# One value projection and stick-breaking rounds in a written order, in the odd layer of a two-layer hybrid trunk

## The chip, the cores and the metric

The kernel runs on one core of one Trainium2 chip. The metric is the device time of one execution in microseconds (us), the median of several runs. The engines have short names here, as in the profile: PE (TensorE, the matmuls), DVE (VectorE), ACT (ScalarE), POOL (GpSimd) and SP (SyncE, which in this kernel issues DMAs only). ACT and POOL issue DMAs as well, each from its own queue.

## The reference

The trunk has two layers on 512 tokens of width 1024. Each is a mixer and a gated ConvFFN, both with a norm before and after and a residual. The change is in the mixer of the second ("odd") layer alone, which runs two kinds of attention side by side, with heads of 64 columns:

```python
def odd_mixer(h, w_in, w_out):
    cq, ck, cv, sq, sk, sv = split_cols(h @ w_in, ODD_SPLITS)   # 768, 768, 768, 256, 256, 256
    ...
    o_dil = dilated_attention(groups(cq), groups(ck), groups(cv), slopes)
    o_sb = stick_breaking_attention(heads_first(sq, SB_HEADS), heads_first(sk, SB_HEADS),
                                    heads_first(sv, SB_HEADS))
    return jnp.concatenate([heads_last(o_dil), heads_last(o_sb)], axis=-1) @ w_out
```

Dilated attention has three groups of four heads. Group 0 looks at a window of 128 tokens with step 1, group 1 at 512 with step 4, group 2 at 2048 with step 16; the three results of a head are merged by their softmax denominators. On 512 tokens, groups 1 and 2 connect tokens of the same residue modulo 4, so the kernel computes them on tokens reordered by residue r.

Stick-breaking attention has four heads. With strict causality it weighs a key by its own probability and by what all the keys between it and the query have left over, a reversed running sum:

```python
        z = jnp.einsum('bhqd,bhkd->bhqk', qblk, k).astype(jnp.float32) * scale
        log_beta = jax.nn.log_sigmoid(z)
        log_keep = jnp.where(strict, jax.nn.log_sigmoid(-z), 0.0)
        after = lax.cumsum(log_keep, axis=3, reverse=True) - log_keep
        a = jnp.where(strict, jnp.exp(log_beta + after), 0.0)
        return jnp.einsum('bhqk,bhkd->bhqd', a.astype(v.dtype), v)
```

## The kernel before

**Products in three parts.** All large products are made of float32 operands split in two: a high part (a cast to the fp32r type) and a low part (the difference). `mm3` (L316 to L320) makes three matmuls of them: high by high, high by low, low by high. A projection over the width of 1024 thus takes 8 k-steps (`KD`) of three matmuls.

**Weights.** The class `Weights` (L42 on) carries the list of all weight units in the order of their use (L207 to L216 for this layer), each 128 x 1024 float32. `load` (L54) issues the DMA of the next unit on SP's queue into one of three raw buffers (`wraw`). `split` (L82) casts it to `wh` on ACT (L83) and subtracts it into `wl` on DVE (L84); there are five buffers of each. `next` hands out the next pair and first sees to it that `depth` units from the present one are made; `ahead` makes units up to a given one. When a raw buffer is used again, its DMA waits in SP's queue until both readers of the earlier tile are done. A second instance `W2` handles the first two units of the output projection, with buffers of its own and the same raw buffers.

**Banks.** PSUM has eight banks, in tags: "a" three, "s" two, "t", "o" and "n" one each. `bank(tag, name)` takes the next of a tag and waits for the readers of its earlier use.

**Order.** Inside a `tc.manual_schedule` block the named engines run their instructions in the order in which the code writes them. Outside, a list scheduler places each instruction by its own estimate of when it becomes ready. SP is in none of the blocks of this function.

**The stages of `odd` (L1424 on), in order of time:**

1. The v12 projection (L1485 to L1504): values of groups 1 and 2, four row tiles of 128 tokens (order 3, 2, 1, 0), each 8 k-steps with 512 columns. ACT copies a finished tile to `vst`, and four DMAs on ACT's own queue scatter its rows by residue into `cv12`. Pieces of the layer before (`pending`) stand between its k-steps.
2. The projections of `sq` and `sk`, stick-breaking's queries and keys, transposed: `proj_T` (L1457), four units of 8 k-steps with 512 columns.
3. `proj_V(sv)` (L1467): stick-breaking's values, four row tiles with 256 columns, two units.
4. Two stick-breaking passes, each for a pair of heads (L1522 to L1600), with the eight projections `T12` of the dilated queries and keys of groups 1 and 2 among them, four in each pass. A pass has scores (PE, L1532), the mask's addition (DVE, L1536), min, Exp, Ln and max (L1542 to L1549), the split of the result in `sh` and `sl` (L226 and L227), and three rounds per head, j = 2, 1, 0. In a round PE adds the block sums into `run` (L1561) and the triangular sums into another bank `cp`, and DVE adds both to z (L1569, L1571); Exp follows for the finished columns on ACT (L1574). Last come the values (`osb`, L1580) and their split. There is one `sh` and one `sl`, so the two heads of a pass use them in turn. This stage stands outside any manual block.
5. In a manual block: the last four T-projections, with the scores of groups 1 and 2 (`score12`) between them; the exchange of softmax tops and sums through DRAM, on SP's queue (`exchange`).
6. `proj_V(cv)`: values of group 0, four row tiles with 256 columns, two units, with group 0's scores (`score0`) between.
7. The values stage: eight items, four of group 0 (`turn0`, `value0`) and four of groups 1 and 2 (`turn12`, `value12`). A turn transposes the softmax weights on PE (L1728) and ACT copies them to a buffer `pt` (L1729); the values add them up in the `oT` banks (L1677). `turned_to` picks the buffer for `pt` from three by the item's own number, so that both `turn0(0)` and `turn12(0, 0)` take the first. From the fifth turn of the loop on, `W.ahead` makes units ahead here: the last two of the output projection and three of the FFN's first.
8. The output projection (`ao`), a loop over four row tiles, with the norms and the FFN's transposes (`turned`) in it.

POOL meanwhile adds up the FFN's weights by accumulating DMAs (`make_sums`), from the end of stage 1 on.

Of the kernel before, what the change touches and what calls it, by code (L numbers as in the profile page):

```python
# [97 lines left out]
def trunk(tc, A, out):  # L98
# [3 lines left out]
    with ExitStack() as top:  # L102
# [1323 lines left out]
        def odd(xnT, pending, order):  # L1426
            xh, xl = xnT
            with ExitStack() as es:
# [4 lines left out]
                cv12 = ap.tile([P, 4, 512], F32, tag="cv12", name="cv12")  # L1433
# [8 lines left out]
                spare = [ap.tile([P, 4, 256], F32, tag=f"spare{n}", name="spare") for n in range(2)]  # L1442
# [4 lines left out]
                sv = sb.tile([P, NT, 256], F32, tag="sv", name="sv")  # L1447
# [4 lines left out]
                def proj_T(dst, scale, permuted, on_act):  # L1452
                    acc = bank("a", "apt")
                    wh, wl = W.next()
                    for k in range(KD):
                        mm3(acc[:], wh[:, k * P:(k + 1) * P], wl[:, k * P:(k + 1) * P],
                            xh[:, k], xl[:, k], k == 0, k == KD - 1)  # L1457
                    src, d = acc[:], dst[:]
# [3 lines left out]
                    if on_act:  # L1462
                        ACT.activation(d, src, AF.Copy, scale=scale)
                    else:
                        DVE.tensor_scalar(d, src, scale, None, ALU.mult)

                def proj_V(dst):  # L1467
                    ws = [W.next() for _ in range(2)]

                    def tile_V(i):  # L1470
                        t = slice(i * P, (i + 1) * P)
                        a = bank("a", "apv")
                        for k in range(KD):
                            wh, wl = ws[k // 4]
                            c = slice((k % 4) * 256, (k % 4 + 1) * 256)
                            mm3(a[:, :256], xh[:, k, t], xl[:, k, t], wh[:, c], wl[:, c], k == 0, k == KD - 1)
                        if i % 2:
                            DVE.tensor_copy(dst[:, i], a[:, :256])
                        else:
                            ACT.copy(dst[:, i], a[:, :256])  # L1480
# [5 lines left out]
                ws = [W.next() for _ in range(4)]  # L1486
                W.depth = 5
                for i in ORDER:
                    t = slice(i * P, (i + 1) * P)
                    a = bank("a", "av12")  # L1490
                    at, *parts = pending.pop(0) if pending else (KD, )
                    for k in range(KD):
                        if k == at:
                            for f in parts:
                                f()
                        wh, wl = ws[k // 2]
                        c = slice((k % 2) * 512, (k % 2 + 1) * 512)
                        mm3(a[:], xh[:, k, t], xl[:, k, t], wh[:, c], wl[:, c], k == 0, k == KD - 1)
                    if not pending:
                        W.ahead(W.pos + 1)  # L1500
                    st = chp.tile([P, 512], F32, tag="s", name="vst")
                    ACT.copy(st[:], a[:])
                    for r in range(4):
                        nc.scalar.dma_start(cv12[32 * i:32 * i + 32, r], st[r::4, :])  # L1504
# [6 lines left out]
                ACT.copy(lead[0:1, 1:2], st[0:1, 0:1])  # L1511
# [6 lines left out]
                tile_V = proj_V(sv)  # L1518
                for i in ORDER:
                    tile_V(i)  # L1520
# [3 lines left out]
                def sb_scores(u):  # L1524

                    zs = [sb.tile([P, 1280], F32, tag="z", name="z", bufs=2) for _ in range(2)]
                    for n, (j0, o0, o1) in enumerate(spans):
                        zp = [bank(t, "zp") for t in ("ss", "nt", "aa")[n]]
                        for j in (j0,) if j0 < 2 else (2, 3):
                            for y in range(2):  # L1530
                                r = slice(y * 64, y * 64 + 64)
                                PE.matmul(zp[y][:, off[j] - o0:off[j + 1] - o0], sk[u][r, j * P:(j + 1) * P],  # L1532
# [416 lines left out]
```

## Time and profile before

| What | us |
|---|---|
| Median of three runs | 1118.72 |
| The three runs | 1118.53, 1118.72, 1124.62 |
| The profiled execution | 1120.18 |
| Its span, first to last instruction | 1118.1 |
| Span of stages 1 to 8 (568.35 to 775.15) | 206.80 |
| Stage 1, v12 projection | 24.51 |
| Stage 5, last T-projections and scores | 27.07 |
| Stage 6, cv projection and scores of group 0 | 16.37 |
| Stage 8, output projection | 22.69 |

The profile is of one execution. The page gives busy time by engine first, then the span in 40 slices, the DMA queues, the chain of work that ended last, and the costliest groups of instructions; the trace answers finer questions, such as busy time by stretch, the waits of an engine, or its instructions in order of time. "L1561" is line 1561 of the kernel before. In a row of the timeline, what stands in square brackets is the idle time before it and what ended it. `out<-in` are the program's names. Matmuls are pipelined and their ends are modelled, so a busy PE may hold short waits.

### The profile page before, as it was taken

To read this page: it belongs to the slowest core of one execution; us is meant where nothing else is said; L and a number is where in the kernel's file an instruction comes from. 1 tells how busy PE (TensorE), PEld (TensorE's weight loads), DVE (VectorE), ACT (ScalarE), POOL (GpSimd) and SP (SyncE) were. 2 spreads that over 40 slices of the span, in tenths; PEclk is the share of its full clock that TensorE was granted. 3 is DMA by queue.
4 is the path that set the end of the run, shared out by engine and by line. 5 is a ranking of instruction groups with operands and counts; after the bars stand their busy time and mean duration, and the time that the engine had idled before them with its cause. 6 is when DMAs were issued, how large, how long until landed. Compare 5 with 4: busy or idle time off the path is not lost.

```text
span 1118.1 us, 18149 instructions
## 1 busy us (share of the span) xinstructions
PE 1105.9 (99%) x6792; PEld 961.6 (86%) x6792; DVE 898.6 (80%) x1509; ACT 641.9 (57%) x1091; POOL 126.2 (11%) x241
## 2 busy tenths in 40 slices
PE   9999999999999999999999999999999999999997
PEld 8876667898999999887888877888999999988876
DVE  6667676488899999999874566677899999999896
ACT  5555576346666665556543554565466666656562
POOL 2311143320000000000032111013200000000002
PEclk9999999999999999999999999999999999999999
DMA  8788898457556555354738999947656565535461
GB/s 289 239 227 228 224 283 219 126 181 199 170 180 196 173 187 180 123 179 150 245 95 280 289 293 289 238 115 201 201 155 199 173 187 191 173 126 164 151 207 75
DMA packets 72599, 218.02 MB, mean 195 GB/s; under 512 B 10048, under 2 KB 11200, under 8 KB 64320
## 3 DMA queue, kind: packets, MB, share of 16 engines
q1 hardware_dynamic: 61248, 147.53, 39.9%
q0 software_dynamic: 9920, 67.12, 24.0%
q10 hardware_dynamic: 1344, 2.23, 0.6%
q8 instruction: 53, 0.87, 0.3%
q14 instruction: 34, 0.28, 0.1%
HBM read 209.47 MB, written 73.43 MB: 253 GB/s over the span
## 4 chain that ended last, share of the span: by engine, by line
PE 76%; DMA 10%; DVE 8%; issue 4%; ACT 1%; POOL 1%; SPq 0%; POOLq 0%; DVEq 0%; ACTq 0%
PE u L320 12%; PE u L318 12%; PE u L319 12%; DMA ws<-in_ffn_up_q 5%; DVE wl L84 3%; DMA ws<-ws 3%; PE apt L318 3%; PE apt L319 3%; PE apt L320 3%; PE acc L318 3%; PE acc L320 2%; PE acc L319 2%; PE ao L318 2%; PE ao L320 2%; PE ao L319 2%
## 5 line engine op out<-in xcount | busy, mean ns | idle before, releaser
L84 DVE TENSOR_TENSOR wl<-wraw,wh 128x1024 fp32r<-128x1024 f32 x246 | 298.8, 1220 | 39.8 <-ACT wh L83 39.0
L83 ACT CAST wh<-wraw 128x1024 fp32r<-128x1024 f32 x246 | 254.8, 1047 | 111.8 <-PE u L319 24.4
L320 PE MATMUL u<-xh,wl 128*128 128x256 f32 (+1 forms) x640 | 195.0, 305 | 0.0
L318 PE MATMUL u<-xh,wh 128*128 128x256 f32 (+1 forms) x640 | 194.9, 305 | 0.0
L319 PE MATMUL u<-xl,wh 128*128 128x256 f32 (+1 forms) x640 | 194.8, 304 | 0.0
L320 PEld LDWEIGHTS u<-xh,wl 128*128 128x128 f32 x640 | 122.3, 191 | 5.5 <-DVE wl L84 0.7
L319 PEld LDWEIGHTS u<-xl,wh 128*128 128x128 f32 x640 | 122.3, 191 | 5.0
L318 PEld LDWEIGHTS u<-xh,wh 128*128 128x128 f32 x640 | 122.3, 191 | 4.9
L318 PE MATMUL u<-gh,wh 128*128 128x256 f32 x384 | 108.7, 283 | 0.0
L320 PE MATMUL u<-gh,wl 128*128 128x256 f32 x384 | 108.6, 283 | 0.0
L319 PE MATMUL u<-gl,wh 128*128 128x256 f32 x384 | 108.6, 283 | 0.0
L318 PE MATMUL acc<-wh,gh 128*128 128x512 f32 (+1 forms) x234 | 90.5, 389 | 0.6 <-DVE uu L689 0.6
L319 PE MATMUL acc<-wl,gh 128*128 128x512 f32 (+1 forms) x234 | 90.9, 388 | 0.0
L320 PE MATMUL acc<-wh,gl 128*128 128x512 f32 (+1 forms) x234 | 90.7, 387 | 0.0
L233 POOL TENSOR_TENSOR rv<-ms,epst 128x1 f32<-128x1 f32 x39 | 12.8, 329 | 632.2 <-ACT junk L285 287.0
L482 ACT ACTIVATE y<-u,cw 128x512 f32<-128x512 f32 x88 | 67.8, 777 | 26.8 <-PE u L320 26.8
L319 PEld LDWEIGHTS u<-gl,wh 128*128 128x128 f32 x384 | 73.7, 192 | 0.1
L318 PEld LDWEIGHTS u<-gh,wh 128*128 128x128 f32 x384 | 73.6, 192 | 0.1
L320 PEld LDWEIGHTS u<-gh,wl 128*128 128x128 f32 x384 | 73.7, 192 | 0.0
L163 POOL DMA_DIRECT2D ws<-in_ffn_up_q x72 | 51.6, 718 | 161.8 <-DMA ws<-ws 75.0
L488 DVE SCALAR_TENSOR_TENSOR y<-u,cw,y 128x510 f32<-128x510 f32 x88 | 65.6, 747 | 2.2
L486 DVE SCALAR_TENSOR_TENSOR y<-u,cw,y 128x511 f32<-128x511 f32 x88 | 65.1, 744 | 0.9 <-ACT y L482 0.9
(374 smaller groups left out, 2495.6 us busy)
## 6 DMA issues: line engine op xcount, KB each, us to landing
ws<-in_ffn_up_q POOLq DMA_DIRECT2D x48, 768.0 KB, 12.3
wraw<-ws SPq DMA_DIRECT2D x128, 256.0 KB, 3.0
wraw<-in_ffn_up_q SPq DMA_DIRECT2D x96, 256.0 KB, 2.9
wraw<-in_ffn_w_down SPq DMA_DIRECT2D x44, 512.0 KB, 3.5
ws<-ws POOLq DMA_DIRECT2D x16, 768.0 KB, 14.2
ws<-in_ffn_up_q POOLq DMA_DIRECT2D x24, 512.0 KB, 6.2
wraw<-in_ffn_w_up SPq DMA_DIRECT2D x24, 512.0 KB, 4.5
wraw<-in_od_w_dqk SPq DMA_DIRECT2D x12, 512.0 KB, 10.3
```

The source lines that it names most:

```text
L83: self.nc.scalar.copy(h[:, :w], raw[:, :w])
L84: self.nc.vector.tensor_tensor(l[:, :w], raw[:, :w], h[:, :w].bitcast(F32), ALU.subtract)
L163: nc.gpsimd.dma_start(tiles[j][c][:].rearrange(wide, q=4), src.rearrange(wide, q=4), accum_op=op, max_dma_last_dim=8192)
L233: POOL.tensor_tensor(v[:, :n], ms, epst[:, :n], ALU.add)
L318: PE.matmul(o, lh, rh, start=first, stop=False, skip_group_check=more)
L319: PE.matmul(o, lh, rl, start=False, stop=False, skip_group_check=more)
L320: PE.matmul(o, ll, rh, start=False, stop=last, skip_group_check=more)
L482: ACT.activation(y[:, z], u[z], AF.Identity, bias=c[:, 3:4], scale=c[:, 2:3])
L486: DVE.scalar_tensor_tensor(y[:, z, 1:], u[z][:, :S - 1], c[:, 1:2], y[:, z, 1:], ALU.mult, ALU.add)
L488: DVE.scalar_tensor_tensor(y[:, z, 2:], u[z][:, :S - 2], c[:, 0:1], y[:, z, 2:], ALU.mult, ALU.add)
```

## The change

It does four things, all in `odd`.

**One projection for the values that aren't strided.** The weight layout joins cv's and sv's columns in units of 512 columns. Stage 1 becomes this joint projection; ACT copies each tile's halves to `cv` and `sv`, and no DMA follows. Stage 3 is gone. Stage 6 becomes the v12 projection, with its copies to `vst` on ACT, and its sixteen scattering DMAs on SP's queue. `cv12` is taken only after the stick-breaking passes.

**Stick-breaking passes in a written order.** Stage 4 is now in a manual block for PE, DVE and ACT, and a function `stick(u)` writes each pass for both heads side by side: both Exp, then both Ln; both casts, then both differences; in each round both heads' products, then both heads' additions. The second head has its own `sh` and `sl`, in the memory of `cv12` and of `spare`, which are free at that time. The running sums have the banks "t" and "o". The T-projections become generators of single k-steps, and `fill(n)` puts n of them at a place: 8 after the Ln, 15 after the splits, 2, 2 and 5 after the rounds. Weights are made ahead at set points.

**Turned buffers by order of taking.** `turned_to` counts its calls, so that the fifth turn takes the second buffer of three and not the first again.

**Raw tiles and splits.** Ahead of stage 6, three raw tiles are asked for (`w.load()`: one of `W2`, two of `W`, the output projection's). The values stage makes only the output projection's two units; three of the FFN's are made in the output projection's loop, one each in its first three turns, and `W.depth` stays 0 until that loop ends.

```diff
-        units += [(A["od_w_v12"][u], 1024) for u in range(4)]
+        units += [(A["od_w_v"][u], 1024) for u in range(4)]
         units += [(A["od_w_sqk"][u], 1024) for u in range(4)]
-        units += [(A["od_w_v"][1, u], 1024) for u in range(2)]
         units += [(A["od_w_dqk"][u], 1024) for u in range(4, 12)]
         units += [(A["od_w_dqk"][u], 1024) for u in range(4)]
-        units += [(A["od_w_v"][0, u], 1024) for u in range(2)]
+        units += [(A["od_w_v12"][u], 1024) for u in range(4)]
...
-                cv12 = ap.tile([P, 4, 512], F32, tag="cv12", name="cv12")
+                sv = ap.tile([P, NT, 256], F32, tag="sv", name="sv")
...
-                def proj_T(dst, scale, permuted, on_act):
+                def T_parts(dst, scale, permuted, on_act):
                     acc = bank("a", "apt")
...
+                        if k < KD - 1:
+                            yield
...
-                ws = [W.next() for _ in range(4)]
+                tile_V = proj_V()
                 W.depth = 5
                 for i in ORDER:
-                    t = slice(i * P, (i + 1) * P)
-                    a = bank("a", "av12")
                     at, *parts = pending.pop(0) if pending else (KD, )
-                    for k in range(KD):
-                        if k == at:
-                            for f in parts:
-                                f()
-                        wh, wl = ws[k // 2]
-                        c = slice((k % 2) * 512, (k % 2 + 1) * 512)
-                        mm3(a[:], xh[:, k, t], xl[:, k, t], wh[:, c], wl[:, c], k == 0, k == KD - 1)
+                    a = tile_V(i, at, parts)
                     if not pending:
                         W.ahead(W.pos + 1)
-                    st = chp.tile([P, 512], F32, tag="s", name="vst")
-                    ACT.copy(st[:], a[:])
-                    for r in range(4):
-                        nc.scalar.dma_start(cv12[32 * i:32 * i + 32, r], st[r::4, :])
+                    ACT.copy(cv[:, i], a[:, :256])
+                    ACT.copy(sv[:, i], a[:, 256:])
...
-                tile_V = proj_V(sv)
-                for i in ORDER:
-                    tile_V(i)
...
+                T12 = [T_parts(t[x], (-0.125, 1.0)[t is ck], True, t is cq) for x in range(2, 6) for t in (cq, ck)]
+                fills = [f for part in T12 for f in [part] * KD]
+
+                def fill(n):
+                    for _ in range(n):
+                        next(fills.pop(0))
+                        if len(fills) % KD == 0:
+                            W.ahead(W.pos + 4)
+
+                def stick(u):
...
+                    W.ahead(W.pos + 5)
+                    for y in range(2):
+                        ACT.activation(sps[y], sps[y], AF.Exp)
+                    for y in range(2):
+                        ACT.activation(sps[y], sps[y], AF.Ln, bias=1.0)
+                    fill(8)
+                    shs = [sb.tile([P, 1280], F32R, tag="sh", name="sh"),
+                           ap.tile([P, 2048], F32R, tag="cv12", name="sh")[:, :1280]]
+                    sls = [sb.tile([P, 1280], F32R, tag="sl", name="sl"),
+                           ap.tile([P, 2048], F32R, tag="spare", name="sl")[:, :1280]]
+                    for y in range(2):
+                        DVE.tensor_tensor(sps[y], zs[y][:], sps[y], ALU.max)
+                        ACT.copy(shs[y][:], sps[y])
+                    for y in range(2):
+                        DVE.tensor_tensor(sls[y][:], sps[y], shs[y][:].bitcast(F32), ALU.subtract)
+                    fill(15)
+
+                    run = [bank(t, "run") for t in "to"]
...
+                        cps = []
+                        for y in range(2):
+                            for part in (shs[y], sls[y]):
+                                PE.matmul(run[y][:, (j + 1) * P:], tri[:, 1], part[:, off[j + 1]:off[j + 2]],
+                                          start=(j == NT - 2 and part is shs[y]), stop=(part is sls[y]),
+                                          skip_group_check=True)
+                            cp = bank(("sn", "ns", "ss")[j][y], "cp")
+                            for i in (3, 2) if j == 2 else (j, ):
+                                o, m = 256 * (i == 3), S - i * P
+                                for part in (shs[y], sls[y]):
+                                    PE.matmul(cp[:, o:o + m], tri[:, 0], part[:, off[i]:off[i] + m],
+                                              start=(part is shs[y]), stop=(part is sls[y]))
+                            cps.append(cp)
+                        for y, z in enumerate(zs):
+                            DVE.tensor_tensor(z[:, c + P:c + n], z[:, c + P:c + n], run[y][:, (j + 1) * P:], ALU.add)
+                        for y, z in enumerate(zs):
+                            DVE.tensor_tensor(z[:, c:c + w], z[:, c:c + w], cps[y][:, :w], ALU.add)
+                            if j < 2:
+                                e = slice(c, 1280 if j else off[1])
+                                ACT.activation(z[:, e], z[:, e], AF.Exp)
+                        fill(2 if j else 5)
...
...
+                    return lambda: split(oS[0][:, u], oS[1][:, u], o)
...
+                with tc.manual_schedule(engines={PE.engine, DVE.engine, ACT.engine}):
+                    depth, W.depth = W.depth, 0
+                    left = stick(0)
+                    left()
+                    left = stick(1)
+                    left()
+                    W.depth = depth
...
+                cv12 = ap.tile([P, 4, 512], F32, tag="cv12", name="cv12")
+                spare = ap.tile([P, 2, 4, 256], F32, tag="spare", name="spare")
...
-                def turned_to(n):
-                    tag, pool = (("spare0", ap), ("spare1", ap), ("sl", sb))[n % 3]
-                    return pool.tile([P, 4, 256], F32, tag=tag, name="pt")[:]
+                taken = []
+
+                def turned_to():
+                    n = len(taken)
+                    taken.append(n)
+                    if n % 3 == 2:
+                        return sb.tile([P, 4, 256], F32, tag="sl", name="pt")[:]
+                    return spare[:, n % 3]
...
-                    tile_V = proj_V(cv)
+                    for w in (W2, W, W):
+                        w.load()
+                    project = proj_V()
+
+                    def tile_V(i):
+                        a = project(i)
+                        st = chp.tile([P, 512], F32, tag="s", name="vst")
+                        ACT.copy(st[:], a)
+                        for r in range(4):
+                            nc.sync.dma_start(cv12[32 * i:32 * i + 32, r], st[r::4, :])
...
-                        if n > 3:
-                            W.ahead(W.pos + n - 1 if n < 7 else 0)
+                        if n == 4:
+                            W.ahead(W.pos + 2)
...
-                W.depth = depth
...
+                        if n < 3:
+                            W.ahead(W.pos + 1 + n)
...
+                W.depth = depth
```

More of the change, by code (lines that the diff above doesn't have):

```diff
@@ L1535, in sb_scores @@
                             for j in (j0,) if j0 < 2 else (2, 3):
[L1536 removed]
+                                DVE.tensor_tensor(zs[y][:, off[j]:off[j + 1]], zp[n][y][:, off[j] - o0:off[j + 1] - o0],
                                                   smask[:, :S - j * P], ALU.add)
[L1539 to L1544 removed]
@@ L1545, in sb_scores @@
[L1545 to L1557 removed]
+                        DVE.tensor_scalar(sps[y], zs[y][:], 40.0, None, ALU.min)
@@ L1563, in sb_weights @@
-                        zp = bank("ssn"[j], "cp")
-                        for i in (3, 2) if j == 2 else (j, ):
-                            o, w = 256 * (i == 3), S - i * P
-                            for part in (sh, sl):
-                                PE.matmul(zp[:, o:o + w], tri[:, 0], part[:, off[i]:off[i] + w],
-                                          start=(part is sh), stop=(part is sl))
-                        DVE.tensor_tensor(z[:, c + P:c + n], z[:, c + P:c + n], run[:, (j + 1) * P:], ALU.add)
```

88 lines of the change are left out of this document (27 added, 61 removed).

## The prediction

> **What bounds the kernel now.** I read the page's busy table first, then busy time by stage, then the chain of waits inside the stages that change, then the queues of ACT and DVE there. The busy table:
>
> ```profile
> PE 1105.9 (99%) x6792; PEld 961.6 (86%) x6792; DVE 898.6 (80%) x1509; ACT 641.9 (57%) x1091; POOL 126.2 (11%) x241
> ```
>
> TensorE (PE) is busy 99% of a span of 1118.1 us. Only two things can shorten it: fewer or cheaper matmuls, or the removal of places where PE waits between them. The diff touches the odd layer's mixer alone. Its stages, PE alone (columns: stretch, length, PE busy with its instructions, granted clock, DMA share, GB/s):
>
> ```profile
> core 0: us, PE busy (x), PEclk, DMA share, GB/s
> 592.86:614.62 21.76, 21.76 (x97) 1.00 0.89 305
> 614.62:626.22 11.60, 11.60 (x97) 1.00 1.02 370
> 626.22:659.05 32.83, 31.88 (x158) 1.00 1.03 245
> 659.05:691.11 32.06, 31.89 (x158) 1.00 1.02 280
> 734.55:752.46 17.91, 17.91 (x188) 1.00 0.50 145
> 626.22:628.58 2.36, 2.36 (x18) 1.00 1.11 208
> 645.05:646.91 1.86, 1.86 (x13) 1.00 1.00 247
> 654.48:654.82 0.34, 0.34 (x3) 1.00 1.10 253
> 656.53:659.05 2.52, 2.52 (x18) 1.00 1.07 267
> ```
>
> The first row is the four projections of sq and sk: 96 matmuls of 512 columns in 21.76 us, 0.227 us each. The second is the sv projection: 96 matmuls of 256 columns in 11.60 us, 0.121 us each. The next two are the stick-breaking passes, one for each pair of heads; then the values of the dilated attention. The last four are pieces of the first pass: the scores, one head's rounds but for its last product, that product, and the values. The clock is granted in full throughout, so a term of PE's time can be moved between stages at the same price.
>
> **The merged projection.** Before, sv (96 matmuls of 256 columns), v12 (96 of 512) and cv (96 of 256) are three projections. After, cv with sv is one of 96 at 512, and v12 another: 96 matmuls fewer, the same columns. Removed 2 x 11.60, added 21.76: **-1.44 us**. Nothing else is saved there; the evictions stay in number and lie under the next matmuls, on ACT (57% busy).
>
> The Trainium skill ("TensorE: Matmul & The Clock Gate", section "Back-to-back issue gap") gives a matmul of N columns N/2.4 + 2.5 ns, which is 215.8 ns and 109.2 ns here; by it the merge would be worth 96 x 2.5 ns, an estimate of 0.24 us. The rows above show 227 and 121 ns, a fixed part of some 15 ns and not 2.5, so the measurement decides.
>
> **The stick-breaking passes.** A pass of before without any wait is: scores 2.36, four T-projections of 24 matmuls (96, so 21.76 by the first row), rounds 2 x (1.86 + 0.34) = 4.40, values 2.52; together 31.04. The passes took 32.83 and 32.06, so 1.79 and 1.02 us are waits, 2.81 in all. Where they come from, in the waits (engine and line, what ended the wait; total, times, longest) and in ACT's queue (start, duration, what ran, idle before it and its releaser):
>
> ```profile
> ACT sh L226 <- PE run L1561: 4.2, 2, 2.1
> ```
> ```profile
> 634.90 0.58 ACT L1463 ACTIVATE cq<-apt 128x512 f32<-128x512 f32 x1
> 635.38 1.04 ACT L83 CAST wh<-wraw 128x1024 fp32r<-128x1024 f32 x1
> 636.43 1.28 ACT L1548 ACT_TABLE_LOAD   x1
> 637.73 2.44 ACT L1548 ACTIVATE sp<-sp 128x1280 f32<-128x1280 f32 x2
> 640.56 1.27 ACT L226 CAST sh<-sp 128x1280 fp32r<-128x1280 f32 x1 [0.40 <-DVE sp L1549]
> ...
> 645.79 1.05 ACT L83 CAST wh<-wraw 128x1024 fp32r<-128x1024 f32 x1 [3.01 <-DMA wraw<-in_od_w_dqk]
> ...
> 649.43 1.27 ACT L226 CAST sh<-sp 128x1280 fp32r<-128x1280 f32 x1 [2.09 <-PE run L1561]
> ```
>
> The second head's cast into sh waits for PE to finish with the first head's, since there is one sh and one sl; and a cast standing 3.01 us before a raw weight tile holds what is behind it. The change gives the second head its own pair of tiles, in memory that is free then, so the first wait has nothing left to wait for. In its written order PE does the scores, 69 T-matmuls (8 and 15 k-steps of three), then the rounds of both heads with 6, 6 and 15 between. Is the chain beside it short enough? DVE and ACT in the second pass:
>
> ```profile
> 663.56 1.55 DVE L1542 TENSOR_SCALAR sp<-z 128x1280 f32<-128x1280 f32 x2
> 669.47 1.49 DVE L1549 TENSOR_TENSOR sp<-z,sp 128x1280 f32<-128x1280 f32 x1 [4.35 <-ACT sp L1548]
> 670.88 1.22 DVE L84 TENSOR_TENSOR wl<-wraw,wh 128x1024 fp32r<-128x1024 f32 x1
> 672.07 1.49 DVE L1549 TENSOR_TENSOR sp<-z,sp 128x1280 f32<-128x1280 f32 x1
> 673.48 1.49 DVE L227 TENSOR_TENSOR sl<-sp,sh 128x1280 fp32r<-128x1280 f32 x1
> ```
>
> DVE's adds and minima end at 663.56 + 1.55, which is 6.06 after the pass began at 659.05. Behind them come one Exp (1.2, as one of the two Ln of that size), the table load 1.28, both Ln 2.44, then for the second head max 1.49, cast 1.27 and difference 1.49, and one more difference between: 6.06 + 1.2 + 1.28 + 2.44 + 5.74 = 16.7. PE reaches the rounds at 2.36 + 69 x 0.227 = 18.0. The chain is hidden by 1.3; a weight pair queued among it (1.04 on ACT, 1.22 on DVE) still just fits.
>
> What is late next is in the rounds. By the columns that they multiply (1024, 1280 and 1792 for each head) the three rounds of both heads (4.40) split about 1.1, 1.4, 1.9. A T-projection ends between the first round and the second, at about 18.0 + 1.1 + 0.7 = 19.8; the weight pair asked for there puts on ACT 0.58 and 1.04, on DVE 1.22, and DVE's adds of the second round stand behind it, at
>
> ```profile
> L1569 DVE TENSOR_TENSOR z<-z,run 128x256 f32<-128x256 f32 x4 | 1.7, 418 | 0.0
> ```
>
> 0.42 for each head. They end at 19.8 + 2.84 + 0.84 = 23.5. PE wants the last round, which writes over what they read, at 18.0 + 1.1 + 1.36 + 1.4 + 1.36 = 23.2: a wait of 0.3. With 0.16 for what I can't see (an estimate, half of that), a pass takes 31.5. Bounds: 31.04 with no wait, 32.83 if nothing is gained. Saved: 1.33 + 0.56 = **-1.89**.
>
> **The values stage.** Chain of waits (start, duration, PE's work):
>
> ```profile
> 743.98 1.29 PE oT L1677 x16
> ...
> 746.29 1.02 PE oT L1677 x16
> ...
> 749.37 0.43 PE ao L318
> ...
> 751.51 1.02 PE oT L1677 x14
> ```
>
> Value groups of 16 matmuls take 1.02 unhindered; the one at 743.98 takes 0.27 more. From 749.37 to 751.51 + 1.02 stand 16 value matmuls (1.02; the last 14 are the row at 751.51) and, left out but for the first, six of the out-projection (6 x 0.227 = 1.36): 0.78 is wait. The first goes with the rotation of the turned buffers by order of taking. The second goes with the three weight splits (ACT 1.04, DVE 1.22 each) that leave this stage, where they stand among the copies of the turned weights. Against that the fifth and sixth turns now share ACT with two other casts, some 0.15. Together **-0.9**, bounds -1.05 and 0.
>
> **Moved.** Those three splits go to the out-projection loop: 3 x 1.22 on DVE, 3 x 1.04 on ACT, under 96 matmuls of 0.227 = 21.8 us. Cover gone, DVE would hold the first FFN matmul; I take +0.2, bounds 0 and 1.2 (one split in full). Sixteen strided DMAs leave ACT's queue for SP's (POOL's is untouched), behind three raw tiles asked ahead and, for the last eight, behind the exchange of softmax sums; costed at nothing, because
>
> ```profile
> L1504 ACTq DMA_DIRECT2D cv<-vst x16: 474/604/616, 576.0 to 595.5; - x16
> ...
> DMA to landing us min/median/max: 2.0/4.2/5.3
> ```
>
> the last tile's copy (0.58, as an eviction of that size above), four issues of 0.60 and the longest landing, 5.3, make 8.3, and the first group of values that reads them is the one at 743.98, 9.4 after the last projection tile ended at 734.55. 1.1 is left.
>
> **Sum.** -1.44 - 1.89 - 0.9 + 0.2 = -4.03. The profiled execution took 1120.18 (span 1118.1 and 2.1 around it), 1.46 over the median of 1118.72; applied to it 1116.15, to the median **1114.7**.
>
> **Rivals.**
>
> First, the rounds stay as they were: a weight pair between two rounds replaces the old wait in full. For: DVE, 80% busy, serves both. Against: 0.3 by the working above. 1118.72 - 4.03 + 1.89 = 1116.6.
>
> Second, all waits go: -1.44 - 2.81 - 1.05 = -5.3, 1113.4. Against: the 0.3.
>
> Third, a raw tile comes late in a pass. Landings between 597 and 704 us, first raw tiles by SP, then POOL's sums of weights, which share the DMA engines (share 1.02 to 1.03 in the passes):
>
> ```profile
> DMA to landing us min/median/max: 4.0/11.1/16.5
> ```
> ```profile
> DMA to landing us min/median/max: 3.6/17.9/24.7
> ```
>
> The tightest raw tile of the new order is asked for when a raw buffer comes free behind the minima, about 6 us into a pass, and its split is wanted in the last fill, at 22 to 24: 16 to 18 later (an estimate from the written order). At 11.1 or 16.5 it is in time; at POOL's 24.7 it is 6.7 or more late: 1114.7 + 6.7 = 1121.4.
>
> Fourth, ending on the other side: the strided pieces on SP's queue land like raw tiles. Decided at 5.3 + 1.1 = 6.4 us from the last issue. At a median of 11.1 PE stands 4.7 before the first strided values: 1119.4. For: raw tiles asked ahead are on that queue just before. Against: POOL's sums are over by then, and these are small. The Trainium skill ("DMA: Bandwidth & Descriptors", section "Queues, rings and completion order") has each hardware queue consumed in ring order, which speaks for this rival: pieces behind 512 KB tiles wait for them. By the page's table of queues this kernel's SP and ACT have a ring each; no row yet shows one delaying the other.
>
> Fifth, what is saved is given back at the start of the FFN or in its weight order, no effect: 1118.7.
>
> **Numbers.** Forecast 0.52, rounds unchanged 0.16, all waits gone 0.11, late raw tile 0.07, late strided values 0.09, no effect 0.05. A change under 1%, 11.2 us, is about what this measurement can't tell from none; no case reaches that. Faster by over 1% 0.02, within 0.94, slower by over 1% 0.04 (strided values at 16.5, 1124.8, with something else late). Range 1111.5 to 1121: below, all waits gone less the runs' own scatter (1118.53 to 1118.72 and one of 1124.62); above, both late cases.
>
> **What would show it.** One value projection at 21.76 before sq and no 256-column one; passes of 31.5 and no ACT cast of sh that waits for PE's run; a value stage without a wait at the first strided group. Wrong if a pass exceeds 32, if PE's first strided group waits for a DMA, or if the first FFN matmuls wait for DVE's wl.

## The result and the profile after

| | Before | After |
|---|---|---|
| Median, us | 1122.28 (7 runs, 1118.53 to 1124.62) | 1113.91 (7 runs, 1112.81 to 1116.67) |
| Profiled execution; its span | 1120.18; 1118.1 | 1114.30; 1112.5 |

The ratio is 0.9947, with a 95% interval of 0.9932 to 0.9963: 5.9 us of 1120, between 4.1 and 7.6. The two medians lie further apart, 8.4 us: the seven runs of the kernel before fall into two groups, 1118.5 to 1119.0 and 1122.3 to 1124.6, and their median is in the upper one. With 21 to 35 runs, beside the experiments, its median was 1119.8 to 1120.6. The page's busy table after:

```profile
PE 1100.5 (99%) x6696; PEld 955.4 (86%) x6696; DVE 894.9 (80%) x1505; ACT 643.2 (58%) x1095; POOL 127.3 (11%) x241
```

PE has 96 matmuls fewer and 5.4 us less to do, and stays at 99%. Its time in the changed stages (columns as in the prediction; in order: value projection, sq and sk, two passes, last T-projections, v12 with scores, values with the out-projection up to its third tile's transposition, the rest of the out-projection, the FFN's first 100 matmuls):

```profile
core 0: us, PE busy (x), PEclk, DMA share, GB/s
567.34:591.84 24.50, 24.50 (x121) 1.00 0.40 125
591.84:613.70 21.86, 21.86 (x98) 1.00 0.90 329
613.70:644.79 31.09, 31.09 (x157) 1.00 1.02 266
644.79:675.96 31.17, 31.17 (x160) 1.00 1.03 288
675.96:702.77 26.81, 26.81 (x162) 1.00 1.03 317
702.77:729.51 26.74, 26.39 (x131) 1.00 0.61 154
729.51:758.49 28.98, 28.98 (x241) 1.00 0.68 197
758.49:769.44 10.95, 10.30 (x54) 1.00 0.65 201
769.44:783.80 14.36, 14.02 (x117) 1.00 0.77 226
sum 216.46, PE 215.12; mean PE 23.90
```

The last three of them in the kernel before, and the sum over its ten stages:

```profile
734.55:765.18 30.63, 30.63 (x242) 1.00 0.64 185
765.18:775.15 9.97, 9.97 (x53) 1.00 0.62 148
775.15:789.14 13.99, 13.96 (x118) 1.00 0.60 177
sum 220.79, PE 219.29; mean PE 21.93
```

So the changed stages are 220.79 - 216.46 = 4.33 us shorter. By part: merge -11.60 + (26.74 - 16.37) + 0.10 = -1.13; passes -1.74 and -0.89; last T-projections -0.26 (0.23 of it is one matmul of theirs that PE did during the second pass, see "The passes"); values -1.65; the rest of the out-projection +0.98, the FFN's start +0.37. The spans differ by 5.6, so 1.3 of it lies in stages that the change doesn't touch; 1.0 of that stands ahead of the first changed matmul (568.35 against 567.34).

What was gained in the values stage is partly given back right behind it. The one wait of PE in the changed stages that is new (what waits, for what; total, times, longest), and POOL's queue in that loop (start, duration, what ran, idle before it and what ended that):

```profile
PE tp L265 <- DVE t L1822: 1.0, 2, 0.7
```
```profile
763.24 0.60 POOL L163 DMA_DIRECT2D ws<-ws  x1 [4.65 <-DMA ws<-in_ffn_up_q]
763.85 0.21 POOL L232 TENSOR_TENSOR rv<-ms,epst 128x1 f32<-128x1 f32 x1
764.14 0.56 POOL L235 TENSOR_TENSOR rr<-rv,mhalf 128x1 f32<-128x1 f32 x1
```

POOL computes the reciprocal roots of the norms (L232, L235) and issues the accumulating DMAs of the FFN's weight sums (L163). The DMA at 763.24 waited 4.65 us for its predecessor; the root behind it, whose mean square ACT had finished at 761.4, came 2.4 us late, DVE's norm with it, and PE stood 0.65 us in the loop.

### The profile page after: what moved, and what is told of

Read it like the earlier page. It is cut to its first block, busy times and chain, and to the rows that moved or that the text cites. A ratio compares the mean times of both kernels' runs of the same rounds, so it can differ in the third digit from the quotient of the medians.

```text
span 1112.5 us, 17970 instructions
## 1 busy us (share of the span) xinstructions
PE 1100.5 (99%) x6696; PEld 955.4 (86%) x6696; DVE 894.9 (80%) x1505; ACT 643.2 (58%) x1095; POOL 127.3 (11%) x241
## 4 chain that ended last, share of the span: by engine, by line
PE 71%; DMA 13%; DVE 8%; issue 5%; ACT 1%; POOL 1%; SPq 0%; POOLq 0%; DVEq 0%; ACTq 0%
PE u L319 12%; PE u L318 12%; PE u L317 12%; DMA ws<-in_ffn_up_q 6%; DMA ws<-ws 3%; DVE wl L84 3%; PE apt L317 3%; PE apt L318 3%; PE apt L319 3%; PE acc L317 3%; PE acc L319 2%; PE acc L318 2%; DMA wraw<-in_ffn_w_down 2%; PE ao L317 1%; DVE wraw L337 1%
## 5 line engine op out<-in xcount | busy, mean ns | idle before, releaser
L318 PE MATMUL u<-xl,wh 128*128 128x256 f32 (+1 forms) x640 | 195.1, 305 | 0.0
L318 PEld LDWEIGHTS u<-xl,wh 128*128 128x128 f32 x640 | 122.4, 191 | 5.0
L318 PE MATMUL u<-gl,wh 128*128 128x256 f32 x384 | 108.8, 283 | 0.0
L318 PE MATMUL acc<-wl,gh 128*128 128x512 f32 (+1 forms) x234 | 91.0, 389 | 0.0
L232 POOL TENSOR_TENSOR rv<-ms,epst 128x1 f32<-128x1 f32 x39 | 13.8, 355 | 629.5 <-ACT junk L284 285.9
L318 PEld LDWEIGHTS u<-gl,wh 128*128 128x128 f32 x384 | 73.8, 192 | 0.1
L163 POOL DMA_DIRECT2D ws<-in_ffn_up_q x72 | 51.6, 718 | 158.9 <-DMA ws<-ws 75.9
## 6 DMA issues: line engine op xcount, KB each, us to landing
ws<-in_ffn_up_q POOLq DMA_DIRECT2D x48, 768.0 KB, 12.3
```

Source lines behind the costliest of these rows:

```text
L163: nc.gpsimd.dma_start(tiles[j][c][:].rearrange(wide, q=4), src.rearrange(wide, q=4), accum_op=op, max_dma_last_dim=8192)
L232: POOL.tensor_tensor(v[:, :n], ms, epst[:, :n], ALU.add)
L318: PE.matmul(o, lh, rl, start=False, stop=False, skip_group_check=more)
```

## The experiments

Times are against the kernel before as run beside each, so ratios compare better across the table than medians do. Stage figures are from the same nine windows.

| Run | Number of runs | Median us | Ratio, 95% interval |
|---|---|---|---|
| same_again | 12 | 1115.48 | 0.9955 [0.9937, 0.9972] |
| splits_back | 12 | 1125.05 | 1.0045 [1.0029, 1.0061] |
| merge_alone | 7 | 1126.73 | 1.0061 [1.0040, 1.0083] |
| merge_moved | 12 | 1118.60 | 0.9991 [0.9978, 1.0005] |
| moves_behind | 6 | 1114.08 | 0.9950 [0.9937, 0.9964] |
| old_passes | 12 | 1116.97 | 0.9973 [0.9956, 0.9989] |
| two_pairs | 10 | 1117.04 | 0.9972 [0.9960, 0.9985] |
| no_written_order | 10 | 1116.45 | 0.9960 [0.9942, 0.9978] |
| less_cover | 12 | 1115.48 | 0.9958 [0.9943, 0.9973] |
| not_ahead | 10 | 1115.72 | 0.9955 [0.9937, 0.9972] |
| roots_free | 5 | 1112.51 | 0.9929 [0.9917, 0.9942] |

### The moved splits

```diff
-                        if n == 4:
-                            W.ahead(W.pos + 2)
+                        if n > 3:
+                            W.ahead(W.pos + n - 1 if n < 7 else 0)
...
-                        if n < 3:
-                            W.ahead(W.pos + 1 + n)
```

> The changed kernel, with the FFN's three weight splits again in the values stage. In the changed kernel's profile the out-projection loop holds one wait of PE for DVE's normed tile (0.65 us, and 0.34 more at the FFN's first transposition). Theory A: that wait comes from POOL, whose reciprocal roots stand behind accumulating DMAs that wait for each other; the raw tiles of the moved splits share the DMA engines with these. Then with the splits back, POOL's DMAs land as before (5.9 us and not 7.8 for the third), the wait shrinks, and the values stage gets its old 0.8 back: within 0.5 us of the changed kernel, so 5 to 6 us under the kernel before. Rival B: the moved splits cost by themselves, as work on DVE and ACT: the whole 1.3 us of the out-projection and the FFN's start goes, and the kernel is some 0.5 us faster than the changed one.

Both theories failed: the kernel is slower than the one before, by 5 us, and 10 to 11 above the changed one. ACT's waits in its values stage, PE's timeline there, and the granted clock by stretch:

```profile
ACT wh L83 <- DMA wraw<-in_ffn_w_up: 8.7, 2, 4.8
```
```profile
749.74 2.45 PE L1681 MATMUL oT<-pt,cv 128*64 128x128 f32 x16 [2.97 <-ACT pt L1738]
...
756.59 2.45 PE L1681 MATMUL oT<-spare,cv 128*64 128x128 f32 x16 [2.95 <-ACT spare L1738]
```
```profile
744.00:747.00 3.00, 2.77 (x22) 1.00 0.87 261
747.00:750.00 3.00, 0.26 (x1) 0.94 1.06 218
750.00:753.00 3.00, 3.00 (x20) 0.50 1.01 251
```

Two casts wait at the head of ACT's queue for raw tiles that were asked for only when the output projection's splits had freed the buffers. The copies of the turned weights stand behind the casts, so PE is idle for 2.97 and 2.95 us. Behind each, the granted clock is 0.50, and 16 value matmuls take 2.45 us, where the same group, at 743.25 in this run, takes 1.09 at full clock: 1.36 more each time, and another 0.42 in the transpositions behind the first. The stage takes 39.71 us, not 28.98. The Trainium skill ("TensorE: Matmul & The Clock Gate", section "Part 1: The HAM clock gate (the "warmup" mystery)") has the clock fall to half after an idle window of about 3.4 us; here idle stretches of PE of 2.97 and 2.95 us were enough.

The merge by itself has this edit too, the old passes (their edit is below) and the old rotation and raw order. Its two turned buffers are halves of one tile, and it leaves out the wait that keeps one from being overwritten while it is still read; so the old rotation's wait isn't in its time:

```diff
-                    for w in (W2, W, W):
-                        w.load()
...
+                def turned_to(n):
...
```

> The one value projection alone: the kernel before with cv and sv in one projection and the strided values late by SP's queue, everything else as before. From the rows of 512 and 256 columns 1.44 us less than the kernel before, 1.2 by the two profiles' stages. By the rule of a gap of 2.5 ns for each matmul, 0.24 us. If the late strided values are waited for, the gain is gone.

It falls into the same waits (values stage 40.06 us). With v12 late, four units pass through the raw buffers ahead of the values and not two, and the FFN's first raw tile is asked for 8 us into that stage; in the kernel before the first two were asked for at 711.3 and 716.9, 23 and 18 us ahead of it. The changed kernel asks as late as that too (737.83, 8.3 us into the stage), but there the first cast of that tile comes at 751.17, behind the values. Then the merge with the splits moved, and with its turned buffers two tiles again:

```diff
+                        if n == 4:
+                            W.ahead(W.pos + 2)
...
+                        if n < 3:
+                            W.ahead(W.pos + 1 + n)
```

> The one value projection alone, with nothing else of the change but the FFN's three splits moved into the out-projection loop: the passes, the rotation of the turned buffers and the order of raw tiles are those of the kernel before. With the splits in the values stage the same projection took 40.1 us for values and the first part of the out-projection, with casts that waited for raw tiles at the head of ACT's queue. Theory A: the move is what the merge needs; then that stage takes 29 to 30 us (0.3 of it the old rotation's wait) and the kernel is 2 to 3.5 us under the kernel before. Rival: the raw tiles asked ahead are needed too; then waits of 3 us or more for a raw tile remain there, and the kernel is slower than before.

Theory A holds for the stage: 29.86 us, with no wait for a raw tile. By the ratio the kernel is 1.0 us under the one before (2.0 by the medians), and the interval, 2.5 less to 0.6 more, takes in no change and little of the 2 to 3.5 expected; its untouched first part took 573.24 us in the profile, 4.9 more than before's. The move is what the merge needs. The raw tiles asked ahead aren't:

```diff
-                    for w in (W2, W, W):
-                        w.load()
```

> The changed kernel without the three raw tiles asked ahead of the last value projection. If they are needed, ACT's casts of the output projection's weights wait for them in the values stage, and values with the first part of the out-projection take 29.6 us (as with the merged projection alone, less the old rotation's 0.27) or more, in place of 28.98. If not, 28.98 again and no difference in time.

The stage took 28.94, the time is that of same_again.

### POOL's queue

```diff
-                        if moves:
-                            moves.pop(0)()
...
+                    while moves:
+                        moves.pop(0)()
```

> The changed kernel, with POOL's last three accumulating DMAs of the FFN's weight sums issued behind the out-projection loop and not one in each of its turns; the moved splits stay where they are. Theory A (POOL's queue holds the roots): the wait of PE for the normed tile, 0.65 us in the loop, is gone, and the stage is 0.8 to 1.0 us shorter than in the changed kernel; 6 to 6.6 us under the kernel before unless the late sums are missed in the FFN. Rival B (the splits hold DVE and ACT): the wait stays at 0.5 to 0.7 us and the time is that of the changed kernel.

> The changed kernel once more, nothing edited. What it tells apart: whether the wait of PE for the normed tile in the out-projection loop (0.65 us in the first profile) stands in every execution, or comes and goes with the landing of one of POOL's accumulating DMAs (7.8 us there, 5.9 in the kernel before, 6.2 with the old passes, where there was no wait). If it is a race of these two, the loop (from its third tile's transposition to the FFN's first matmul) takes anything between 9.94 and 10.95 us; if it is the splits, 10.95 again. The stages from the value projection to the FFN's start should be within 0.5 us of the first profile otherwise, and the part ahead of them, which the change does not touch, may stray by some us (567.3 to 571.9 us so far).

With the DMAs behind the loop, it took 9.94 us and the FFN's start 14.19. But so it did in the second profile of the changed kernel:

```profile
762.73:772.67 9.94, 9.94 (x53) 1.00 0.70 227
772.67:786.71 14.04, 13.91 (x118) 1.00 0.70 205
```

The DMA that landed after 7.8 us in the first profile landed after 6.2 here. So the wait is a race, lost in one of these two executions. The other profiles with the splits moved and the DMAs in the loop agree. Counted from the start of the loop's window, that DMA landed at 4.4 us in the first profile and at 3.7 in not_ahead, where the loop took 10.95 and 10.27; in the other six, same_again among them, it landed at 2.3 to 2.8 and the loop took 9.94 to 9.97. moves_behind by itself shows no gain in the median. Without the race, the window shows no cost of the moved splits in that loop.

### The passes

```diff
-                with tc.manual_schedule(engines={PE.engine, DVE.engine, ACT.engine}):
-                    left = stick(0)
...
+                for u in range(2):
+                    zs = sb_scores(u)
...
```

> The changed kernel, with the stick-breaking passes of the kernel before (one pair of tiles, list scheduler), and the rest of the change. If the written order with its second pair of tiles is worth what the stages of the two profiles show, the passes take 32.8 and 32.1 us again and the time is 2.6 us above the changed kernel, some 3 us under the kernel before. Rival: the stages of one profiled execution differ by chance, and the time is within 0.8 us of the changed kernel.

Its passes take 32.03 each, not 32.8 and 32.1. The median is 1.5 us above same_again's, 2.0 by the ratios, not the 2.6 expected. The 0.8 that is missing was in the kernel before by chance, as that kernel shows when it is run once more, unedited:

> The kernel before, once more. Its first pass took 32.83 us and its second 32.06; behind the merged projection both old passes took 32.03. If the 0.8 is the raw weight tile that a cast waited 3.01 us for, and that is due to the old order of the units, the first pass takes 32.8 again. If it is a chance landing, it takes some 32.0.

```profile
627.46:659.54 32.08, 31.88 (x158) 1.00 1.03 245
...
734.99:766.96 31.97, 30.68 (x242) 1.00 0.64 180
```

The first pass takes 32.08 this time, and no cast waits for a dqk raw tile. The values stage, in turn, takes 31.97, 1.3 more than in the first profile: there a cast waits 2.0 us for a raw tile of the FFN, and PE 1.3 for the turned weights behind it. That is the wait of splits_back, by chance in the kernel before. So single late landings move by a microsecond from stage to stage.

Is it the tiles, the order, or how the code is written? First the code of the change with its manual block taken away, then the old passes with the second pair of tiles:

```diff
-                with tc.manual_schedule(engines={PE.engine, DVE.engine, ACT.engine}):
+                with ExitStack() as _:
```

> The changed kernel, with the code of its passes as it is (second pair of tiles, heads side by side, k-steps as fill) but outside a manual block, so that the list scheduler sets the order. If the second pair of tiles is what counts, the passes take 31.1 us each as in the changed kernel. If the written order counts, they take 32.0 or more, like the old passes behind the merged projection, and the time is 1.7 us or more above the changed kernel.

```diff
-                    sh = sb.tile([P, 1280], F32R, tag="sh", name="sh")
+                    sh = (ap.tile([P, 2048], F32R, tag="cv12", name="sh")[:, :1280] if y
+                          else sb.tile([P, 1280], F32R, tag="sh", name="sh")[:])
...
```

> The changed kernel with the passes of the kernel before (list scheduler, one head after the other), but with a second pair of tiles for the second head's split. If the single pair is what cost the old passes (32.03 each behind the merged projection), they take 31.1 or less here. If what counts is that both heads' steps are written side by side, they stay at 31.8 to 32.0.

The passes of the first, and then of the second:

```profile
617.60:648.50 30.90, 30.90 (x157) 1.00 1.02 281
648.50:679.45 30.95, 30.95 (x158) 1.00 1.02 291
```
```profile
617.42:649.62 32.20, 31.56 (x158) 1.00 1.02 280
649.62:681.58 31.96, 31.80 (x158) 1.00 1.02 279
```

Neither the tiles alone nor the written order: with both heads' steps written side by side, with k-steps as fill, the list scheduler does as well as the manual block. That form needs the second pair of tiles, as both heads' splits are alive at once. No run had it with one pair. Nor do the runs part the order of the heads from what comes with it: the k-steps as fill, the weights made at set points, and a bank for each head's running sum. two_pairs has one such bank for both heads, and PE's longest wait in its passes, 0.6 us, is for DVE's addition out of it.

The prediction's cover:

```diff
-                    fill(15)
+                    fill(11)
...
-                        fill(2 if j else 5)
+                        fill(2 if j else 9)
```

> The changed kernel, with four k-steps of T-projection (12 matmuls, 2.72 us) taken from ahead of the rounds and put behind the last round: 8 and 11 ahead, 2, 2 and 9 behind the rounds. By the prediction's working PE would then reach the rounds at 15.3 us into a pass while the chain on DVE and ACT takes 16.7: a wait of 1.4 us in each pass, 2.8 in all. By the changed kernel's profile the second head's difference is ready 16.1 us into the pass and PE gets to it at 16.1 too: no wait there; and the third T-projection then ends behind the last round, so that the weight pair that now stands ahead of DVE's additions in the second round comes later, and a pass gets 0.2 to 0.5 us shorter.

No wait of that size appeared: the passes took 30.87 us and 31.01. DVE's queue in the changed kernel's second pass (begun at 644.79) shows why, and shows the predicted wait behind it:

```profile
658.01 2.89 DVE L1556 TENSOR_TENSOR sl<-sp,sh 128x1280 fp32r<-128x1280 f32 x2
...
666.79 1.23 DVE L84 TENSOR_TENSOR wl<-wraw,wh 128x1024 fp32r<-128x1024 f32 x1 [1.55 <-ACT wh L83]
667.93 0.75 DVE L1577 TENSOR_TENSOR z<-z,run 128x256 f32<-128x256 f32 x2
```

The second head's difference is ready at 660.90, 16.1 into the pass (16.7 predicted), and PE gets to that head 0.7 behind the first one. The additions of the second round end at 668.68, 23.9 into the pass (23.5 predicted), behind the weight pair; the first of the two, 0.42 long, ends at 668.35. PE's timeline at that place:

```profile
668.27 0.39 PE L317 MATMUL apt<-xh,wh 128*128 128x512 f32 x1
668.50 0.34 PE L1566 MATMUL run<-sh,tri 128*128 128x384 f32 x1
```

PE was ready for the last round at 668.27, 23.5 into the pass (23.2 predicted), and the addition whose operand the round's first product writes over ended 0.1 later. PE filled the gap with one matmul: the seventh of this fill of six, and the first of the projections behind the passes, which begin with their second one (L318, 675.96) and take 26.81 us, not the 27.04 of no_written_order. So the second pass without it is 31.17 - 0.23 = 30.94. In the first pass PE waited 0.1 at the same place.

### A version with POOL's roots free

In the layer that the change doesn't touch, the part ahead of the change took 567.3 to 573.2 us in the profiles, and most of the difference arises between 144 us and the layer's FFN, which begins at 228 to 235. There POOL's first roots stand behind the last step of a chunk of sums. In same_again the two DMA rows show in brackets their waits for the DMA before:

```profile
136.92 0.54 POOL L163 DMA_DIRECT2D ws<-ws  x1 [8.77 <-DMA ws<-in_ffn_up_q]
142.92 0.79 POOL L163 DMA_DIRECT2D ws<-in_ffn_up_q  x1 [5.46 <-DMA ws<-ws]
143.44 0.37 POOL L1208 MEMSET epsp<- 128x1 f32 x1
```

PE waited 2.2 us there for what follows from it, and from 147.08 to 150.48 its granted clock was 0.50. That parts the profiles in two: in seven (same_again, splits_back, merge_moved, moves_behind, two_pairs, no_written_order and not_ahead) this wait is 2.0 to 3.8 us, the clock is at half for 3.4 us behind it, and the untouched part takes 571.1 to 573.2; in the other six (the two of the kernel before, the changed kernel's first, merge_alone, old_passes and less_cover) the wait is 0.9 to 2.1, the clock stays whole, and the part takes 567.3 to 569.6. So this version issues that step three values later, beside the edits of moves_behind and less_cover:

```diff
-                        make_sums(0, range(2, 3), sums_of[0][3][1][0:1, 0:1])
+                        held = sum_steps(0, range(2, 3), sums_of[0][3][1][0:1, 0:1])
+                        with tc.manual_schedule(engines={POOL.engine}):
+                            for move in held[:-1]:
+                                move()
...
+                            if n == 4:
+                                held[-1]()
```

> A version meant to beat the changed kernel: its edits are the accumulating DMAs behind the out-projection loop, the 8 and 11 k-steps ahead of the rounds, and one edit in the first layer: the last step of POOL's third chunk of weight sums, which waits for its predecessor at 141 to 145 us of the span while POOL's first reciprocal roots stand behind it, is issued three values later. If the scatter of the part that the change does not touch (567.3 to 573.2 us in the profiles so far) comes from that place, this part takes 567 us or less, the wait of PE for DVE's combined weights there (1.0 to 3.8 us) goes, and the runs lie closer together, with a median 2 to 4 us under the changed kernel's, 8 to 10 under the kernel before. If it comes from elsewhere, it stays between 567 and 573 and the median is within 1 us of the changed kernel's.

```profile
134.88 0.53 POOL L163 DMA_DIRECT2D ws<-ws  x1 [7.04 <-PE o L1273]
135.40 0.12 POOL L1211 MEMSET epsp<- 128x1 f32 x1
135.83 0.18 POOL L1279 TENSOR_TENSOR st<-st,epsp 128x1 f32<-128x1 f32 x1 [0.31 <-POOL epsp L1211]
```

The root comes at 135.83, PE's wait there is gone, the clock stays whole, and the untouched part takes 566.64 us. The changed stages take 215.11, as in same_again (215.14), so by the profiles what is gained lies in the untouched part. The median, 1112.51, is 3.0 under same_again's and 7.5 under that of the kernel before beside it (1120.0; 8.0 by the ratio). It is the lowest of all, though its interval overlaps with those of the changed kernel. The five runs lie within 1.1 us (1111.74 to 1112.83), where the changed kernel's twelve, in same_again, spread over 8.1. Five runs are few: five of moves_behind's six lie within 1.3 us as well, and its sixth, the profiled one, has the half clock. The edit in the first layer was not timed by itself; moves_behind and less_cover, alone, were within a microsecond of same_again's ratio. The Trainium skill ("DMA: Bandwidth & Descriptors", section "Anatomy of one DMA — SWDGE (gpsimd) path") has a DMA's wait on a semaphore happen on the sequencer that issues it, ahead of the issue; POOL's rows agree: what stands behind in its program stood for 4.65 to 8.77 us.

## The prediction against the runs

**The sum.** Forecast was 4.03 us less, to 1114.7; by stages the two pairs of profiles give 4.3 (before and after) and 221.29 - 215.14 = 6.2 (before_again and same_again), by the first ratio 5.9. The forecast is at the low end: just outside the interval of that ratio (4.1 to 7.6) and inside that of same_again (3.1 to 7.1). That the first pair comes within 0.3 of it is luck. Term by term the merge brought 0.3 less than forecast, the passes with the last T-projections 1.0 more, the values stage 0.75 more, and the moved splits cost 1.15 more.

**The merged projection** was right in mechanism: -1.13 to -1.15 for -1.44 (and not the 0.24 of the other estimate given there); the 96 matmuls of v12 with the scores between took 10.37 more than cv's, not 10.16.

**The passes** came out near the number, for a reason that was half wrong. The sum took all of 1.79 us in the first pass as a cost of the old form; 0.75 of it was one late raw tile (before_again has 32.08). In its place the passes fell below the forecast 31.5, to 31.09 and 30.94: the unhindered pass, 31.04, was put together from pieces that held waits themselves. Its values took 2.52 and in the new form take 2.30. The forecast wait of 0.3 ahead of the last round is there, at 0.1. The reason given, one sh and one sl, is not enough: two_pairs keeps the old time.

**The values stage** was mis-sized: -0.9, with -1.05 as its bound, against -1.65 and -2.98. The step counted waits on the chain between 743.98 and 752.53 alone. The first transpositions (2.04 us in the old profile, 1.84 in the new) and the out-projection's matmuls behind 752.53 (54 in 12.72 us, where 54 x 0.227 is 12.3) held the rest. Of the 2.98, 1.3 is the late raw tile of before_again.

**The moved splits** are the step that failed in kind. The prediction costed them as work that leaves one stage and enters another, +0.2. splits_back and merge_alone show that the late v12 needs the move: without it the raw tiles come too late and the merge loses 7 us. What it costs in the loop and the FFN's start, against the first profile of the kernel before, came out as +1.35 in one execution and +0.02 in another, by way of POOL's queue, which the prediction held untouched because none of its instructions move. Whether the raw tiles that moved beside it made POOL's DMA late is open: in same_again they lie beside it as well, and it landed after 6.2.

**The strided values** were costed rightly at nothing. By SP's queue they land in

```profile
DMA to landing us min/median/max: 1.9/2.1/3.1
```

less than the 4.2 of before. Why is not shown; neither a raw tile nor one of POOL's sums was under way (the last had landed at 717.5 and 717.7, the first piece was issued at 718.3), so the rival of pieces that wait behind raw tiles was not put to the test. The last piece was there at 734.2, 4.5 ahead of the first values that read it. The rivals of a late raw tile in a pass and of unchanged rounds did not come about, nor did any of the three signs of being wrong: no pass over 32, no wait for a DMA at the first strided values, none for DVE's `wl` at the first FFN matmuls.

## What to carry to other kernels

A stage's excess in one profile is not yet what a change can win: profile the kernel before a second time, since single late landings move by a microsecond from stage to stage. When a projection moves, follow the shared raw buffers from its new place on, and ask which cast will stand at the head of an engine's queue waiting for a transfer; in splits_back two idle stretches of PE of 3 us cost a further 3 at half clock. Small computations that PE waits for do not belong behind DMA issues that wait for one another.

## What the runs showed of the hardware

Three microseconds of idle PE were followed by a granted clock of one half for about the next three (0.94, then 0.50 in the windows above). In the first layer a wait of 2.0 us was followed by it in one profile (not_ahead) and a wait of 2.1 in another (before_again) was not. A POOL accumulation landed after 7.8 us in one execution and 6.2 in the next, in the same place of the same program. And with one such DMA no longer ahead of a root, beside two other edits, five runs spread over 1.1 us where twelve had spread over 8.1.
